# Router of a mixture of experts: the low parts of the tokens on VectorE alone, and fillers that read results of the ranking

## The chip, the cores and the metric

The kernel runs on one core of a Trainium2 chip. The metric is device time in microseconds (us) of one execution, as the median of several runs. Five engines work side by side, each through its own queue in order: TensorE (PE; its weight loads are PEld), VectorE (DVE), ScalarE (ACT), GpSimd (POOL) and SyncE (SP, which issues the DMAs).

## The reference, cut to what matters

Two blocks are computed one after the other on 256 tokens of 1024 features. The second block has two layers, and each layer ends with a mixture of 16 experts:

```
scores = sigmoid(t @ router_w);  biased = scores + router_bias
grp_score = sum of the two best biased scores in each of 4 groups of 4 experts
sel_group = argmax(grp_score);   top_idx = the two best experts in that group
gates = the unbiased scores of the two, divided by their sum
y = sum over experts of gates * (silu(gate) * up) @ w_down      (float32)
x = layer_norm(alpha * x + y)
```

The change lies in the router and in the gathers behind it. Both run once for each layer.

## The kernel before, in words

Products need float32 accuracy. An operand is split into a high part (`xnh`) and a low part (`xnl` = x - `xnh`), and each token is multiplied as high and low part.

The router is in `moe`. The normalised tokens stand in `zn`, [128 tokens, 2 token blocks t, 1024 features]. ACT makes the sigmoid's exponential, and then VectorE ranks in a chain of small instructions: `rank` over the experts of a group (`ed`, `erk`), the two best (`gs`, which is `found`), their sum by group (`gsc`, which is `summed`), `rank` over the four groups (`gd`, `grk`) and the selection `selb`. Three products on TensorE (lines 1406 to 1408, into the PSUM tile `po`) count the place of each token in the list of its expert, and VectorE makes from them `posm` and the slot matrices `sm`, one for each token block.

`to_gather` makes the operands of the gathers meanwhile: for each half c of the features and each t, ACT normalises `zn` (line 1364) and rounds it to `xnh` (1365), and one engine makes `xnl` (1366): GpSimd for c = 0, VectorE for c = 1. `first_ready` traces these four steps behind the slot matrices; its `issue_after` orders only instructions that stand on the same engine as the one it names. Behind them in program order stands `gates_and_rounds`: VectorE's `w` and `ws` (the gates), two products of TensorE into a further column range of `po` (1423, 1424), and `cmx`, VectorE's maximum of that (1426).

Each `gather` is eight products of 256 columns, `xnh` and `xnl` of two token blocks for two feature blocks, into one PSUM bank. The banks `st` and `w` have one buffer each and take turns: gather 0 uses `st`, which `po` holds until `cmx` has read it, and gather 1 uses `w`. Gathers 0 and 1 (features 0 to 511, c = 0) stand ahead of the first product of the experts (line 1632); gathers 2 and 3 (c = 1) lie between those products.

`busy(n)` issues n products that nothing reads (fillers, line 370). The router has `busy(30)`, two `busy(20)` and, behind the place products, `busy(14)`, all into bank `w`. None of these fillers waits for a result: the `issue_after` around them names an instruction of VectorE, so it does not order TensorE. The rows of statistics for the residual (line 435) lie between the fillers.

A planner fixes the order of each engine's queue before the run: of the instructions that its own cost figures take to be ready when an engine becomes free, it issues the one that comes first in the program. On the chip each engine works off its queue in that order.

Of the kernel before, what the change touches and what calls it, by code (L numbers as in the profile page):

```python
# [8 lines left out]
F32 = mybir.dt.float32  # L9
# [4 lines left out]
ALU = mybir.AluOpType  # L14
# [16 lines left out]
# ---------------------------------------------------------------- constants  # L31
def _constants():
    """Tables that depend on the shapes alone."""
# [4 lines left out]
    # rotate-half permutation for two stacked heads of 64  # L38
# [9 lines left out]
    # partial sums: rows 0 and 32 of one kind, 64 and 96 of another  # L48
# [26 lines left out]
    # trailing mean minus token, transposed: [token in, token out]  # L75
# [9 lines left out]
    # retention decay with the 1/sqrt(dk) of the keys, [key, query]  # L85
# [9 lines left out]
    # router helpers: iota - 512 over slots; the lead by which f comes before e in a group of four  # L95
# [11 lines left out]
def _cols(v):  # L107
    """[n*128] -> [128, n]: one column per block of 128 features."""
    return np.ascontiguousarray(np.asarray(v).reshape(-1, P).T)


def _panels(w, n):
    """[K, N] -> [N/n, 128, K/128, n], one contiguous block per panel."""
    w = np.asarray(w)
    K, N = w.shape
    return np.ascontiguousarray(w.reshape(K // P, P, N // n, n).transpose(2, 1, 0, 3))


def layout(inputs):
    """Only moves data: every array keeps its type and values."""  # L120
# [27 lines left out]
    pair = [0, 3, 1, 4, 2, 5]      # heads whose keys lie in the first / second half, in turn  # L148
# [24 lines left out]
# ---------------------------------------------------------------- kernel  # L173
def body(tc, A, out, dbg=None, stop=None):
# [3 lines left out]
    with ctx:  # L178
# [22 lines left out]
        # ------------------------------------------------------------ streams  # L201
# [12 lines left out]
        class weights:  # L214
            """fp32 weights [128, kb, n] from DRAM, split exactly into hi + lo, in two halves, of which
            some are made at once and the others when first used."""
# [23 lines left out]
            def at(self, k, a=None, b=None):  # L240
                """hi and lo of block k, columns a to b (all by default)."""
                for i, (k0, k1, c0, c1) in enumerate(self.cut):
                    if k0 <= k < k1 and (a is None or c0 <= a < c1):
                        c = slice(None) if a is None else slice(a - c0, b - c0)
                        return [t[:, k - k0, c] for t in self.make(i)]

        def mm3(o, wh, wl, xh, xl, first, last):
            """o += w^T x, both operands split; only lo*lo (below fp32) is left to rounding."""
# [7 lines left out]
        def xtile(tag, dt=F32R, name=None):  # L256
            """[128, KB, T + 2], or that much of another use."""
            return xp.tile([P, KB * (T + 2)], dt, name=name or tag, tag=tag)

        class Lead:  # L260
            """A tensor's split product with its gains, made block by block as its sums become known: the first
            products of the next step run on it, and what is the same for all features of a token is applied to them.
            Further columns, an even number, hold vectors that are added to each token, so that their products come along.
            The normalised tensor takes its place."""

# [15 lines left out]
            def products(self, ws, banks, ks):  # L281
                """Of the four blocks of columns of two panels, a bank each."""
# [10 lines left out]
        # ------------------------------------------------------------ start  # L293
# [28 lines left out]
        def ada(i):  # L322
            """Column i of the nine modulation vectors, a generator of a step per cut, or of two for the first."""
            mod = mods[:, i * 8:i * 8 + 8]
            for a, b in CUTS if i < 2 else [(a, a + 2) for a in range(0, KB, 2)]:
# [31 lines left out]
                if i % 3 == 1:   # scale: g * (1 + sc)  # L357
                    V.scalar_tensor_tensor(out=mod[:, c], in0=mod[:, c], scalar=1.0,
                                           in1=gains[:, i // 3 * 8 + a:i // 3 * 8 + b], op0=ALU.add, op1=ALU.mult)
                if i % 3 == 2:   # gate: 0.5 of the half steps, 0.5 of the sigmoid gates  # L360
# [5 lines left out]
        def busy(n, tag="w"):  # L366
            """Keeps the clock of the tensor engine up over a wait: products that nothing reads."""
            p = bank(tag, "busy")
            for i in range(n):
                PE.matmul(p[:, :P], identb, identb, start=True, stop=True)  # L370

        # ------------------------------------------------------------ norms
        class Sum:
            """Sums over all features of [128, T] blocks, as a column per token block."""
# [29 lines left out]
        class Norm:  # L404
            """Mean square over features of a transposed [128, KB, T] tensor, block by block."""
# [26 lines left out]
        def rows_to(rb, r):  # L432
            """Per-token columns [128, 2] as a row over all partitions: PSUM [128, T]."""
# [7 lines left out]
        def row(rb):  # L441
            """A row from PSUM in SBUF."""
# [4 lines left out]
        def lead_in(nrm, i, lead, ws, banks):  # L447
            """The first products, and the normalised tensor in place of their operand: rmsnorm(h) * scale + shift."""
# [9 lines left out]
        def norm_mod(rb, h, i, hi, lo):  # L458
            """hi + lo = rmsnorm(h) * scale + shift."""
# [7 lines left out]
        def first_rstd():  # L467
            """1 / rms of the input, as a row."""
# [24 lines left out]
        # ------------------------------------------------------------ FFN  # L493
        def begin(pool, start, pq, i, uh, ul, win):
            """The first three pairs of panels of the first FFN, one or two blocks of K at a time as the modulation comes in."""
# [115 lines left out]
        # ------------------------------------------------------------ rope of block 1  # L611
# [31 lines left out]
        def rotate(dst, src, cosT, sinT, pool, pq, raw=None, n=2):  # L643
            """dst [128, n, T] = rope of the two stacked heads in src, in PSUM unless raw has them too."""
# [10 lines left out]
        def proj_t(o, w, a, xh, xl, kb=KB):  # L655
            """o [128, T] = W[:, a:a+128]^T x^T."""
# [3 lines left out]
        def proj_k(banks, xh, xl, ks=range(KB)):  # L660
            """Several [128, T] products at once, the blocks of K outermost; a bank is a list of (o, w, a)."""
# [5 lines left out]
        def proj_n(o, w, xh, xl, t, kb=KB, k0=0, kt=None, cols=(None, None)):  # L667
            """o [tokens of block t, N] = x W."""
# [12 lines left out]
        def evac(dst, src):  # L681
            """PSUM to SBUF on the engine whose turn it is."""
# [6 lines left out]
        # ------------------------------------------------------------ softmax attention  # L689
        def softmax_rows(sc, n, nk, scale, pool, sink=None):  # L690
            """Joint softmax over [128, n, nk] scores in PSUM, one maximum per query."""
# [11 lines left out]
        # ------------------------------------------------------------ block 1 mixer  # L703
        def mixer(nrm, cosT, sinT, side, lead, then):
            with tc.tile_pool(name="mix", bufs=1, reuse_waits="tile") as pool, tc.tile_pool(name="mixp", bufs=1, reuse_waits="tile", space=bass.MemoryType.PSUM) as pq:
# [40 lines left out]
                # pooling  # L746
# [117 lines left out]
        # ------------------------------------------------------------ block 2  # L864
# [14 lines left out]
        rw = ctile([P, KB, 32], name="rw", pool=c2)     # router weights, and a column of ones for the sums  # L879
# [5 lines left out]
        def shift(means, after):  # L885
            """hT = alpha * hT - mean(alpha * hT)."""
# [9 lines left out]
        class LayerNorm:  # L896
            """Of hT + y, its sums taken on the tensor engine."""
# [10 lines left out]
            def add(self, m, y):  # L908
                """hT[:, m] += y."""
# [14 lines left out]
            def columns(self):  # L924
                """By token: the mean, the mean square, 1 / the deviation, and - the mean times that."""
# [12 lines left out]
            def finish(self, dst, g, b, each):  # L938
                """Block by block: dst = the normalised tensor; hT keeps what it was, less its mean."""
# [14 lines left out]
        def pair_softmax(s, scale, pool, sink=None):  # L954
            """Rows of two heads: s [128, 4, T], a bank per head, late queries in 0 and 2, early ones in 1 and 3."""
# [39 lines left out]
        def pair_values(pq, pool, p, pe, v, hi, lo):  # L995
            """hi + lo [128, T]: outputs of the two heads, transposed; v[i](t) are the values of key block t."""
# [13 lines left out]
        def first_weights(l, which, made=0):  # L1010
            """The first weights of a mixer."""
            return [weights(A["w_in_2"][l, i], KB, 256, "k", made=made) for i in which]

        def mixer2(l, lead, cols, first, normalise):
            with tc.tile_pool(name=f"mix2_{l}", bufs=1, reuse_waits="tile") as pool, \
# [54 lines left out]
                def latent(x, n, i, wc):  # L1070
                    """The rms norm of x, and then its transpose, split."""
# [22 lines left out]
                # latent queries, keys and values  # L1094
# [76 lines left out]
                # retention  # L1171
# [67 lines left out]
                # the router on the normalised sum z + y is linear in it but for the two statistics of a token  # L1239
# [30 lines left out]
                def after(m):  # L1270
                    """Block m of the sum: to token rows, and the products and sums over the features.
                    Blocks 0 to 6 a block in each quarter of the columns, the last one by token at once."""
# [53 lines left out]
        def moe(l, cols, zn, lg, GB, ahead):  # L1326
            col = lambda o, m: cols[:, o + m:o + m + 1]
            with tc.tile_pool(name=f"moe_{l}", bufs=1, reuse_waits="tile") as pool:
# [5 lines left out]
                # statistics of the tokens, and the router's logits  # L1334
# [21 lines left out]
                # the normalised tokens, without gain and shift, for the gathers  # L1356
# [3 lines left out]
                def to_gather():  # L1360
                    for c in range(2):
                        for t in range(2):
# [3 lines left out]
                            (G, V)[c].tensor_tensor(out=xnl[:, t, c_], in0=x, in1=xnh[:, t, c_].bitcast(F32), op=ALU.subtract)  # L1366
# [8 lines left out]
                def rank(x, n, name):  # L1375
                    """How many of the four come before each: larger, or equal and earlier. x [128, n*4]."""
# [24 lines left out]
                with tc.issue_after(found.ins):  # L1401
                    busy(20)
                with tc.issue_after(summed.ins):
                    busy(20)
# [11 lines left out]
                def gates_and_rounds():  # L1416
# [5 lines left out]
                    # more than CAP tokens for an expert: that many further rounds  # L1422
# [10 lines left out]
                with tc.tile_pool(name=f"moep_{l}", bufs=1, reuse_waits="tile", space=bass.MemoryType.PSUM) as pq:  # L1433
# [5 lines left out]
                    def residual_now():  # L1439
                        """hT = alpha * (its normalised value - the mean of that)."""  # L1440
# [61 lines left out]
        def experts(l, big, pool, nb, xn, posm, gates, acc, col, aside=None, loop=None):  # L1502
            """acc += the experts' outputs of the tokens in slots 0 to CAP-1 of each; two experts at a time,
            one in the left and one in the right half of the columns of the tensor engine."""
# [3 lines left out]
            def stage():  # L1508
                """Keeps the tensor engine to the order of the program."""
# [12 lines left out]
            def expert_weights(e, i, n):  # L1522
                """fp32 [128, 4, 512] of the gate and up weights for i = 0, 1; [128, 2, 1024] of the down weights for 2."""
# [298 lines left out]
```

## Time and profile before

| | us |
|---|---|
| median of 3 runs | 1182.7 |
| the three runs | 1182.67, 1182.70, 1187.75 |
| span of the profiled execution, first to last instruction | 1186.2 |
| PE busy | 1144.6 (96%) |
| PEld busy | 943.5 (80%) |
| DVE busy | 713.3 (60%) |
| ACT busy | 511.4 (43%) |
| POOL busy | 44.5 (4%) |

The profile gives the profiled execution's span but no other time of its own. Of the three runs only the one of 1187.75 us is long enough to contain a span of 1186.2 us. Spans count from the first instruction. The router of the first layer lies near 732 to 746 us and that of the second near 1024 to 1039 us. The mean granted clock of TensorE is 0.987, where 1.00 is 2.4 GHz and 0.50 is 1.2 GHz.

### The profile page before, as it was taken

How to read it: one execution, taken by the hardware profiler on the slowest of the kernel's cores; microseconds unless marked ns; L12 is line 12 of the kernel's file. 1: busy time of each engine (PE TensorE's matmuls, PEld its weight loads, DVE VectorE, ACT ScalarE, POOL GpSimd, SP SyncE). 2: the span in 40 equal slices, each digit the busy share in tenths (PEclk: the TensorE clock that was granted, in tenths of full speed). 3: DMA queues.
4: the chain of work that ended last, by engine and by line, in shares of the span. 5: the costliest groups of instructions: out<-in, count | busy, mean ns of one | idle time of the engine just before them, and what ended most of it. 6: DMA issues, size and time to landing. Idle time of an engine off the chain costs nothing. (4 is left out here: it accounts for less than half of the span.)

```text
span 1186.2 us, 20785 instructions
## 1 busy us (share of the span) xinstructions
PE 1144.6 (96%) x8495; PEld 943.5 (80%) x8495; DVE 713.3 (60%) x1410; ACT 511.4 (43%) x946; POOL 44.5 (4%) x53
## 2 busy tenths in 40 slices
PE   6999999999999999999999998999989999899995
PEld 4999999988888999999997878544458787844443
DVE  5698879777877775555677754621258864451114
ACT  4454445534534554444556434222247643322213
POOL 0000001000000200000120001000001000100000
PEclk9999999999999999999999999999989999999998
DMA  9788779738863455535572439599743334779941
GB/s 317 292 362 307 288 258 325 263 133 316 306 230 112 173 180 182 184 125 183 168 250 99 143 109 353 216 385 390 290 155 135 136 109 170 288 272 397 380 156 38
DMA packets 77354, 272.12 MB, mean 229 GB/s; under 512 B 7873, under 2 KB 10817, under 8 KB 62914
## 3 DMA queue, kind: packets, MB, share of 16 engines
q1 hardware_dynamic: 77250, 270.70, 62.8%
q8 instruction: 70, 1.15, 0.4%
q14 instruction: 34, 0.28, 0.1%
HBM read 269.63 MB, written 1.05 MB: 228 GB/s over the span
## 5 line engine op out<-in xcount | busy, mean ns | idle before, releaser
L254 DVE TENSOR_TENSOR hl<-raw,hl 128x1024 fp32r<-128x1024 f32 (+5 forms) x267 | 293.4, 1108 | 120.8 <-ACT hl L254 120.0
L254 ACT CAST hl<-raw 128x1024 fp32r<-128x1024 f32 (+5 forms) x267 | 254.0, 958 | 233.9 <-PE mm L251 172.2
L249 PE MATMUL mm<-xh,hl 128*128 128x256 f32 x896 | 255.2, 286 | 4.0 <-ACT xh L254 3.3
L251 PE MATMUL mm<-xh,hl 128*128 128x256 f32 x896 | 255.2, 285 | 0.0
L250 PE MATMUL mm<-xl,hl 128*128 128x256 f32 x896 | 253.4, 283 | 0.0
L249 PEld LDWEIGHTS mm<-xh,hl 128*128 128x128 f32 x896 | 169.6, 190 | 6.6 <-ACT xh L254 3.6
L250 PEld LDWEIGHTS mm<-xl,hl 128*128 128x128 f32 x896 | 170.4, 190 | 1.9 <-issue 1.9
L251 PEld LDWEIGHTS mm<-xh,hl 128*128 128x128 f32 x896 | 170.4, 190 | 1.0 <-issue 1.0
L1632 PE MATMUL gu<-hl,xg 128*64 128x512 f32 x208 | 101.8, 604 | 0.0
L249 PE MATMUL mm<-gh,hl 128*128 128x256 f32 x352 | 99.2, 282 | 0.0
L251 PE MATMUL mm<-gh,hl 128*128 128x256 f32 x352 | 99.2, 282 | 0.0
L250 PE MATMUL mm<-gl,hl 128*128 128x256 f32 x352 | 99.2, 282 | 0.0
L1632 PE MATMUL gu<-raw,xg 128*64 128x512 f32 x192 | 92.9, 603 | 0.0
L354 DVE SCALAR_TENSOR_TENSOR raw<-raw,cond 128x1024 f32<-128x1024 f32 x64 | 76.7, 1219 | 10.0 <-DMA raw<-in_w_ada_dram 10.0
L1668 DVE SCALAR_TENSOR_TENSOR ysl<-dn,gsl,ysh 128x512 fp32r<-128x512 f32 x32 | 23.9, 750 | 75.8 <-ACT ysh L1667 75.8
L250 PEld LDWEIGHTS mm<-gl,hl 128*128 128x128 f32 x352 | 67.0, 190 | 0.0
L249 PEld LDWEIGHTS mm<-gh,hl 128*128 128x128 f32 x352 | 67.0, 190 | 0.0
L251 PEld LDWEIGHTS mm<-gh,hl 128*128 128x128 f32 x352 | 67.0, 190 | 0.0
L1632 PE MATMUL gu<-rawe,xg 128*64 128x512 f32 x112 | 54.6, 604 | 0.0
L1619 DVE TENSOR_SCALAR xg<-ga,cols 128x256 f32<-128x256 f32 x32 | 17.4, 543 | 55.8 <-ACT xg L1618 55.8
L1667 ACT ACTIVATE ysh<-dn,gsl 128x512 fp32r<-128x512 f32 x32 | 22.0, 687 | 55.7 <-PE dn L1665 55.7
L1618 ACT ACTIVATE xg<-ga,cols 128x256 f32<-128x256 f32 x32 | 18.1, 565 | 60.9 <-PE ga L1615 55.0
(531 smaller groups left out, 2428.3 us busy)
## 6 DMA issues: line engine op xcount, KB each, us to landing
raw<-in_w_ffn_in_dram SPq DMA_DIRECT2D x41, 1024.0 KB, 4.9
raw<-in_w_ada_dram SPq DMA_DIRECT2D x34, 1024.0 KB, 6.2
raw<-in_w_in_dram SPq DMA_DIRECT2D x34, 1024.0 KB, 5.0
hl<-in_gate_up_dram SPq DMA_DIRECT2D x26, 1024.0 KB, 8.5
raw<-in_gate_up_dram SPq DMA_DIRECT2D x24, 1024.0 KB, 7.9
raw<-in_w_ffn_out_dram SPq DMA_DIRECT2D x32, 704.0 KB, 4.2
rawe<-in_gate_up_dram SPq DMA_DIRECT2D x14, 1024.0 KB, 8.2
raw<-in_w_out_dram SPq DMA_DIRECT2D x12, 1024.0 KB, 4.9
```

Of the source, the lines that this page charges most:

```text
L249: PE.matmul(o, wh, xh, start=first, stop=False)
L250: PE.matmul(o, wh, xl, start=False, stop=False)
L251: PE.matmul(o, wl, xh, start=False, stop=last)
L254: return S.copy(hi, x), V.tensor_tensor(out=lo, in0=x, in1=hi.bitcast(F32), op=ALU.subtract)
L354: V.scalar_tensor_tensor(out=w, in0=w, scalar=1.0, in1=cond, op0=ALU.mult, op1=ALU.mult, accum_out=mod[:, a + j:a + j + 1])
L1618: S.activation(out=xg[:, 2 * j], in_=p[:, :T], func=AF.Identity, scale=col(0, 2 * j), bias=col(8, 2 * j))
L1619: mark[0] = V.tensor_scalar(out=xg[:, 2 * j + 1], in0=p[:, T:], scalar1=col(0, 2 * j + 1), scalar2=col(8, 2 * j + 1), op0=ALU.mult, op1=AL ...
L1632: mm = PE.matmul(p[i * CAP:(i + 1) * CAP], xg[:, k, s], w[i][:, k % 4], start=(k == 0), stop=(k == KB - 1))
L1667: made = S.activation(out=ysh[:, c], in_=p, func=AF.Copy, scale=gc)
L1668: mark[0] = made, V.scalar_tensor_tensor(out=ysl[:, c], in0=p, scalar=gc, in1=ysh[:, c].bitcast(F32), op0=ALU.mult, op1=ALU.subtract)
```

## The change

`to_gather` makes all four `xnl` on VectorE. `busy` gets a new argument `since`: with it, the fillers begin with one float32 product of the identity with the tensor named, so that this product waits for the tensor. The two `busy(20)` in the router become one product that reads `gs` with 8 fillers, and one that reads `gsc` with 10, both into bank `st`. `gather` does the products of both feature blocks with `xnh` before those with `xnl`. The rest of the diff takes out comments and docstrings.

```
-        def busy(n, tag="w"):
+        def busy(n, tag="w", since=None):
             p = bank(tag, "busy")
+            if since is not None:
+                PE.matmul(p[:, :since.shape[-1]], ident, since, start=True, stop=True)
             for i in range(n):
                 PE.matmul(p[:, :P], identb, identb, start=True, stop=True)
...
-                            (G, V)[c].tensor_tensor(out=xnl[:, t, c_], in0=x, in1=xnh[:, t, c_].bitcast(F32), op=ALU.subtract)
+                            V.tensor_tensor(out=xnl[:, t, c_], in0=x, in1=xnh[:, t, c_].bitcast(F32), op=ALU.subtract)
...
                 busy(30)
                 with tc.issue_after(found.ins):
-                    busy(20)
+                    busy(8, "st", gs.rearrange("p a b -> p (a b)"))
                 with tc.issue_after(summed.ins):
-                    busy(20)
+                    busy(10, "st", gsc)
...
-                    for i in range(2):
-                        k = 2 * j + i
-                        for h in range(2):
-                            for t in range(2):
+                    for h in range(2):
+                        for t in range(2):
+                            for i in range(2):
+                                k = 2 * j + i
                                 mm = PE.matmul(p[:, i * T:(i + 1) * T], xn[h][:, t, k * P:(k + 1) * P], sm[:, t].rearrange("p e s -> p (e s)"),
-                                               start=(h + t == 0), stop=(h + t == 2))
+                                               start=(h + t + i == 0), stop=(h + t + i == 3))
```

## Rows read from the trace of the kernel before

**Rows 1.** Busy time by engine in five stretches (us, instructions in brackets), granted clock, DMA.
```profile
core 0: us, PE busy (x) PEld busy (x) DVE busy (x) ACT busy (x) POOL busy (x), PEclk, DMA share, GB/s
738.40:741.40 3.00, 0.00 (x0) 0.00 (x0) 2.81 (x6) 2.86 (x5) 2.45 (x2) 1.00 0.33 121
...
743.50:744.95 1.45, 1.45 (x9) 1.45 (x8) 1.45 (x4) 0.00 (x0) 0.00 (x0) 0.50 0.00 0
...
1035.30:1038.50 3.20, 3.16 (x15) 3.19 (x16) 2.41 (x11) 0.56 (x1) 0.00 (x0) 0.50 0.02 5
...
780.00:840.00 60.00, 60.00 (x338) 29.25 (x336) 12.22 (x22) 14.35 (x27) 0.00 (x0) 1.00 1.04 397
...
697.20:700.60 3.40, 2.69 (x18) 1.71 (x18) 0.45 (x2) 0.88 (x3) 1.64 (x1) 1.00 0.35 141
```

**Rows 2.** Timeline of TensorE, first layer: start, length, engine, line, operation, idle before.
```profile
732.92 0.62 PE L1278 MATMUL lgt<-rwg,hT 128*128 128x18 f32 x4
...
734.11 1.22 PE L370 MATMUL busy<-identb 128*128 128x128 bf16 x19
735.17 0.44 PE L435 MATMUL acc<-k_c_mats,nmu 128*128 128x128 f32 x2
735.45 1.28 PE L370 MATMUL busy<-identb 128*128 128x128 bf16 x20
...
741.40 0.17 PE L1406 MATMUL pos<-selb,ltb 128*128 128x16 bf16 x1 [3.01 <-DVE selb L1396]
...
741.48 1.63 PE L370 MATMUL busy<-identb 128*128 128x128 bf16 x14
...
743.51 0.77 PE L1615 MATMUL ga<-sm,xnh 128*128 128x256 f32 x2
...
746.22 0.64 PE L1632 MATMUL gu<-raw,xg 128*64 128x512 f32 x1
```

**Rows 3.** Timeline of TensorE, second layer.
```profile
1033.77 0.17 PE L1406 MATMUL pos<-selb,ltb 128*128 128x16 bf16 x1 [3.01 <-DVE selb L1396]
...
1035.34 0.77 PE L1615 MATMUL ga<-sm,xnh 128*128 128x256 f32 x2 [0.20 <-DVE ws L1418]
...
1038.82 0.64 PE L1632 MATMUL gu<-raw,xg 128*64 128x512 f32 x1
```

**Rows 4.** Timeline of VectorE, first layer.
```profile
738.20 0.19 DVE L1389 SCALAR_TENSOR_TENSOR gs<-erk,bi 128x32 f32<-128x32 f32 x1
...
738.43 0.19 DVE L1391 TENSOR_REDUCE gsc<-gs 128x8 f32<-128x32 f32 x1
738.65 1.03 DVE L1381 TENSOR_TENSOR gd<-gsc 128x32 f32<-128x32 f32 x1
739.71 1.19 DVE L1382 TENSOR_TENSOR gd<-gd,k_c_small 128x32 f32<-128x32 f32 x1
740.94 0.19 DVE L1384 TENSOR_REDUCE grk<-gd 128x8 f32<-128x32 f32 x1
...
741.88 0.76 DVE L1572 TENSOR_TENSOR sm<-k_c_small,posm 128x256 fp32r<-128x256 f32 x2
...
743.19 0.17 DVE L1426 TENSOR_REDUCE cmx<-pos 128x1 f32<-128x16 f32 x1 [0.45 <-PE pos L1424]
743.28 0.18 DVE L1418 TENSOR_REDUCE ws<-w 128x2 f32<-128x32 f32 x1
743.37 0.42 DVE L1572 TENSOR_TENSOR sm<-k_c_small,posm 128x256 fp32r<-128x256 f32 x1
743.70 1.29 DVE L1366 TENSOR_TENSOR xnl<-zn,xnh 128x512 fp32r<-128x512 f32 x2
```

**Rows 5.** Timeline of GpSimd, first layer.
```profile
738.36 2.49 POOL L1366 TENSOR_TENSOR xnl<-zn,xnh 128x512 fp32r<-128x512 f32 x2 [2.75 <-ACT xnh L1365]
```

**Rows 6.** Timeline of ScalarE, first layer.
```profile
737.68 1.12 ACT L1365 CAST xnh<-zn 128x512 fp32r<-128x512 f32 x2
...
740.13 1.12 ACT L1365 CAST xnh<-zn 128x512 fp32r<-128x512 f32 x2
```

**Rows 7.** Timeline of VectorE, second layer.
```profile
1034.92 0.18 DVE L1417 TENSOR_TENSOR w<-sc,selb 128x32 f32<-128x32 f32 x1
```

## The prediction

> **What bounds the kernel now.** I first read busy time by stretches. TensorE is the bound wherever the experts run: in the 60 us from 780 it is busy for all 60.00 at full clock while VectorE needs 12.22 [rows 1]. So a microsecond that the experts start earlier is a microsecond at the end, as long as nothing else holds them. In the router it is different. From 738.40 to 741.40 TensorE does nothing and VectorE, ScalarE and GpSimd are busy for 2.81, 2.86 and 2.45 us [rows 1]. The timeline of TensorE names what ends that wait: the place products at 741.40 had waited 3.01 us for the selection, and the second layer shows the same 3.01 us [rows 2, 3]. What counts is thus how early the first expert product starts, now 746.22 and 1038.82 [rows 2, 3]. On the way to it VectorE is the path: ranking, place products, slot matrices, `cmx`, then the gathers.
>
> Two things in that path are long. The two `gd` instructions, on 32 elements, take 1.03 and 1.19 us, where their neighbours take 0.19 and start 0.22 apart. They end at 739.68 and 740.90. GpSimd runs its two `xnl` from 738.36 to 740.85, so each `gd` ends where one of them does, while `gsc`, a reduction with one input, runs at 0.19 beside them [rows 4, 5]. And the clock falls behind the 3 us wait: 0.50 from 743.50 to 744.95, and 0.50 from 1035.30 to 1038.50 [rows 1], which is 1.2 GHz, in both layers just when the gathers run.
>
> **The change part by part.** All times are those of the first layer; the second lies 292.37 later (1033.77 - 741.40) [rows 2, 3].
>
> *No GpSimd in the ranking.* Both `gd` go to 0.22 apart: 738.65, 738.87, and `grk` at 739.09 instead of 740.94. That is 1.85 us a layer, and the place products could go at 739.55. The bounds are 0 (the wait has another cause) and 1.85.
>
> The Trainium skill, "SBUF — State Buffer", section "Who interferes with whom", says that a VectorE instruction with two SBUF inputs and a GpSimd instruction that reads SBUF exclude each other for the whole instruction. By that rule alone, with nothing else late, the sum would be 2 x 1.85 = 3.7 us less, 1179.0. The rows agree on the lock, but not that nothing else is late.
>
> *Fillers that wait.* Ahead of the place products TensorE now waits for `gs` (738.39, seen by TensorE at about 738.45), then does a float32 product and 8 fillers, then another and 10 fillers. A float32 product costs 0.28 (735.17 to the next start at 735.45; the smaller ones of line 1278 are four records, two products, in 0.62, so the other bound is 0.31). A filler costs 0.056 (19 from 734.11 to 735.17) [rows 2]. Together 0.28 + 0.45 + 0.28 + 0.56 = 1.57, so the place products go at 740.02, not 739.55: queued behind the fillers they lose 0.47 of the 1.85. At half clock the fillers cost double, 3.14. The gain so far is 741.40 - 740.02 = 1.38 us, and the slot matrices, which end at 742.64 now [rows 4], end at 741.26. The 40 fillers that go had run in time that TensorE waited anyway and give nothing back. The move from bank `w` to `st` queues nothing new: the place products use `st` behind them on the same engine.
>
> *Four `xnl` behind the slot matrices.* GpSimd's two go to VectorE at 1.29 for two, so VectorE has 2.58 us of them instead of 1.29 [rows 4]. Where they stand in its queue decides. In program order all four come ahead of `w`, `cmx` and `ws`. Now those three, and even a slot matrix of the next round, stand ahead of the two `xnl`, although `xnh` was ready at 741.25 on the chip [rows 4, 6]; so the planner took the second `xnh` to be ready only about when that slot matrix ran. The new two read the first `xnh`, ready at 738.80 [rows 6]; they come directly behind the slot matrices and fill 1.29 us, longer than the stretch from the end of the slot matrices to the end of that slot matrix in the second layer's order (`w` to gather 0.42, and the slot matrix 0.42 [rows 4, 7]; 0.84 together). By then the planner will hold the second `xnh` ready too, and put all four first. `w` then starts at 741.26 + 2.58 = 743.84. Gather 0 waits for `cmx`, because `po` holds its bank: in the second layer it starts 0.42 after `w` starts (1034.92 to 1035.34 [rows 3, 7]). So gather 0 starts at 744.26, against 743.51 now, and at 1036.63, against 1035.34: 0.75 and 1.29 later than before. The bounds of this part: with `w` first it would start at 741.68, with two `xnl` first at 742.97, with four at 744.26. I take four.
>
> *The gathers.* From gather 0 to the first expert product it is 2.71 us and 3.48 us now, of which 1.44 and 3.15 at half clock [rows 1 to 3]. Half of these is what the clock costs: 0.72 and 1.58. The rest, 1.99 and 1.90, is the price at full clock, 1.95 in the mean. The new order of the eight products in all 32 gathers changes neither their number nor their shapes; with all four `xnl` made before, it gains nothing. No row has that alternation. The two figures for the same two gathers differ by 0.09, 0.045 a gather, so I allow 32 x 0.045 = 1.4 us to either side and take 0.
>
> *The clock.* TensorE ends its fillers, place products and counts at about 741.05 (740.02 plus the 14 fillers, 0.78, plus 0.2) and then waits for gather 0 until 744.26, 3.2 us; now it waits 3.01 and loses the clock each time [rows 2, 3]. So I expect the loss again, right at the gathers. What it costs depends on when the clock falls: the two layers show 0.72 and 1.58, I take the mean, 1.15; the bounds are 0 and 1.95 (all of the gathers at half).
>
> The Trainium skill, "TensorE: Matmul & The Clock Gate", section "What's actually happening", states that the throttled state is the default and that activity releases it; the chip does not align its watch to the start of a program. By that rule the same kernel can pay differently from run to run, anything between the two bounds above; no run here shows it apart.
>
> **The sum.** First layer: 744.26 + 1.95 + 1.15 = 747.36 against 746.22, +1.14. Second: 1036.63 + 1.95 + 1.15 = 1039.73 against 1038.82, +0.91. Together +2.05, all of it passed on, since TensorE is the bound behind. Against the profiled execution's span of 1186.2 that is 1188.3; around it lie about 1.5 us if it was the run of 1187.75. The median of the three runs, 1182.7, is 5.05 less than that run; I put the same +2.05 on it: 1184.8. Its own range, by the clock's bounds, is 1182.4 to 1186.4.
>
> **The rivals.**
> 1. *`cmx` comes between the two pairs of `xnl`.* Gather 0 starts at 742.97, TensorE waits only 1.9 us and may keep its clock; a stretch with some 0.7 us of waiting kept 1.00 [rows 1], and 3 us did not. First expert products at 744.92 and 1037.29: -1.30 and -1.53, 1179.9. For it: the planner's times are its own. Against it: the order argued above.
> 2. *`cmx` comes directly behind the slot matrices, as in the second layer now.* Gather 0 starts at 741.68 on `xnh`; the second `xnl` ends at 741.26 + 0.42 + 1.29 = 742.97, two products (0.24) and gather 1 (0.97) follow: 744.2, and 1036.6. -2.0 and -2.25: 1178.4. Against it: `xnl` of the first half is ready earlier and stands earlier in the program.
> 3. *Slower: the clock falls already before the place products.* The fillers of `busy(30)` end at 735.33; three products of line 435 at 0.28 follow, so TensorE waits from about 736.3 to 738.45, 2.1 us, for `gs`. If that is enough, the fillers cost 3.14, place products go at 741.59, the slot matrices end at 742.83 and gather 0 starts at 745.83. With 1.95 and 1.15: 748.93 and 1041.30, +2.71 and +2.48, in all 1187.9; with all gathers at half clock 1189.5. It decides from the point where a wait of 2.1 us drops the clock, which lies between the waits seen.
> 4. *The ranking is not sped up.* `grk` stays at 740.94, the slot matrices end at 742.64, gather 0 starts at 745.64: with 1.95 and 1.15 it is +2.5 and +2.3, 1187.5. Against it: both `gd` end with GpSimd's instructions.
> 5. *As forecast, but the clock stays up*: 1182.4.
>
> **How the numbers follow.** Forecast 0.45, rival 1 0.23, rival 2 0.08, rival 3 0.09, rival 4 0.04, rival 5 0.11. The range takes in rivals 1 to 4, from 1178.3 to 1188.6; the order of the gathers (1.4) and a clock that is down longer lie in what is left out. A measurement of this kernel tells about 0.5%, 5.9 us, from no change: below 1176.8 lies only rival 2 with more gained from the gathers or the clock, 0.04; above 1188.6 the upper part of rivals 3 and 4, 0.09; between them 0.87.
>
> **What the profile would show.** Both `gd` at about 0.2 us and no `xnl` on GpSimd (else rival 4). Line 370 in two groups of 8 and 10 from 738.45 at 0.056 each (0.11 is rival 3). In VectorE's queue, four `xnl` between the slot matrices and `w` (two: rival 1; none: rival 2). Gather 0 near 744.3 and 1036.6, released by `cmx` or `ws`, and 0.50 in the stretch behind. I would be wrong if gather 0 started ahead of 743, or if the clock stayed at 1.00 through both gathers.

## The result, and the profile after

| | changed | before, in the same session |
|---|---|---|
| median, us | 1190.92 (8 runs, 1188.73 to 1194.44) | 1184.34 (8 runs, 1182.60 to 1188.38) |
| profiled execution, us | 1190.96, span 1189.1 | span 1186.2 |
| mean granted clock | 0.986 | 0.987 |
| GpSimd busy, us | 39.3 | 44.5 |

The ratio of the times is 1.0051, with an interval from 1.0032 to 1.0069: slower by about 6 us. The forecast had the sign right (+2.05) and the size wrong; 1190.92 lies above its range. Two executions, of 2116.95 us (r6) and 2774.26 us (r7), stand far outside all others of their kernels and are left out of the ratios below.

Spans mislead here. The router of the changed kernel begins 3.9 us earlier than that of before (its `gs` starts at 734.33, against 738.20 in [rows 4]), although nothing ahead of it was changed, and still the span is 2.9 us longer. The early clock goes with that: in the profile of before the granted clock is 0.50 from 28.4 to 34.5 us, where the changed kernel's has 1.00. Of the ten traces of this document three, before, e2 and r7, have such a stretch there and reach `gs` at 736.9 to 738.2; the other seven reach it at 733.6 to 734.5. So both traces are compared from `gs` of the first layer on. From there to the end before needs 448.0 us (1186.2 - 738.20) and the changed kernel 454.8 (1189.1 - 734.33): +6.8.

The timeline of VectorE of the changed kernel, first layer, answers to [rows 4]. Its columns are start, length, engine, line, operation, and the idle time before it with what ended that.

```profile
734.33 0.19 DVE L1391 SCALAR_TENSOR_TENSOR gs<-erk,bi 128x32 f32<-128x32 f32 x1
...
734.77 0.19 DVE L1383 TENSOR_TENSOR gd<-gsc 128x32 f32<-128x32 f32 x1
735.00 0.19 DVE L1384 TENSOR_TENSOR gd<-gd,k_c_small 128x32 f32<-128x32 f32 x1
...
735.45 0.19 DVE L1398 SCALAR_TENSOR_TENSOR selb<-grk,top 128x32 bf16<-128x32 f32 x1
736.76 0.19 DVE L1412 SCALAR_TENSOR_TENSOR posm<-selb,pos 128x32 f32<-128x32 bf16 x1 [1.13 <-PE pos L1410]
...
737.67 2.49 DVE L1368 TENSOR_TENSOR xnl<-zn,xnh 128x512 fp32r<-128x512 f32 x4
740.07 0.18 DVE L1419 TENSOR_TENSOR w<-sc,selb 128x32 f32<-128x32 f32 x1
740.18 0.17 DVE L1428 TENSOR_REDUCE cmx<-pos 128x1 f32<-128x16 f32 x1
740.29 0.18 DVE L1420 TENSOR_REDUCE ws<-w 128x2 f32<-128x32 f32 x1
```

Both `gd` take 0.19 us, where [rows 4] has 1.03 and 1.19. The ranking is done at 735.64, but `posm` waits 1.13 us more for TensorE. Then all four `xnl`, 2.49 us, stand ahead of `w`, `cmx` and `ws`.

The timeline of TensorE, first layer, answers to [rows 2]:

```profile
731.58 0.94 PE L372 MATMUL busy<-identb 128*128 128x128 bf16 x14
...
734.58 0.41 PE L370 MATMUL busy<-gs,k_c_mats 128*128 128x32 f32 x2 [1.33 <-DVE gs L1391]
734.82 0.61 PE L372 MATMUL busy<-identb 128*128 128x128 bf16 x8
735.49 0.39 PE L370 MATMUL busy<-gsc,k_c_mats 128*128 128x8 f32 x2
735.73 0.72 PE L372 MATMUL busy<-identb 128*128 128x128 bf16 x10
736.51 0.17 PE L1408 MATMUL pos<-selb,ltb 128*128 128x16 bf16 x1
...
740.49 1.19 PE L1617 MATMUL ga<-sm,xnh 128*128 128x256 f32 x4 [3.29 <-DVE ws L1420]
...
744.17 1.12 PE L1634 MATMUL gu<-raw,xg 128*64 128x512 f32 x1
...
746.83 0.75 PE L1617 MATMUL ga<-sm,xnh 128*128 128x256 f32 x4
```

And of the second layer, which answers to [rows 3]; its `gs` starts at 1030.84:

```profile
1031.08 0.41 PE L370 MATMUL busy<-gs,k_c_mats 128*128 128x32 f32 x2 [1.33 <-DVE gs L1391]
...
1033.30 0.17 PE L1408 MATMUL pos<-selb,ltb 128*128 128x16 bf16 x1
...
1037.29 1.19 PE L1617 MATMUL ga<-sm,xnh 128*128 128x256 f32 x4 [3.28 <-DVE ws L1420]
...
1043.70 0.75 PE L1617 MATMUL ga<-sm,xnh 128*128 128x256 f32 x4
```

The busy time by stretches shows the clock (third figure from the end: 1.00 is 2.4 GHz, 0.50 is 1.2 GHz). The first four stretches are of the first layer, the others of the second:

```profile
core 0: us, PE busy (x) PEld busy (x) DVE busy (x) ACT busy (x) POOL busy (x), PEclk, DMA share, GB/s
737.30:738.90 1.60, 0.00 (x0) 0.00 (x0) 1.60 (x5) 0.09 (x1) 0.00 (x0) 1.00 0.00 0
739.00:740.40 1.40, 0.00 (x0) 0.00 (x0) 1.40 (x6) 0.00 (x0) 0.00 (x0) 0.50 0.00 0
740.50:744.20 3.70, 3.70 (x18) 3.48 (x18) 1.77 (x10) 0.57 (x1) 0.00 (x0) 0.50 0.00 0
744.20:745.70 1.50, 1.50 (x5) 0.50 (x6) 0.54 (x1) 0.57 (x1) 0.00 (x0) 0.50 0.00 0
...
1032.60:1034.00 1.40, 1.07 (x12) 0.74 (x9) 0.40 (x2) 1.29 (x3) 0.00 (x0) 0.50 0.05 18
...
1041.00:1042.70 1.70, 1.70 (x5) 0.50 (x6) 0.54 (x1) 0.56 (x1) 0.00 (x0) 0.50 0.05 10
1042.80:1044.00 1.20, 1.20 (x8) 0.39 (x5) 0.00 (x0) 0.00 (x0) 0.00 (x0) 1.00 0.00 0
```

In the first layer the clock falls while TensorE waits for gather 0 and stays at 0.50 through both gathers and the first two blocks of expert products. In the second it is down already among the waiting fillers at 1032.6, ahead of the place products at 1033.30, and comes back only near 1042.8.

Because the low clock outlasts the gathers, the mark for the comparison is the start of the third gather (746.83 and 1043.70 above), behind the first four expert blocks. From there to the last expert product of the first layer both kernels take 127.51 us, so nothing of the router reaches further, and the new order of the gathers' products costs and gains nothing there. The 6.8 us are then:

| stretch | before | changed | difference |
|---|---|---|---|
| first layer, `gs` to third gather | 9.89 | 12.50 | +2.61 |
| last product of layer 1 to `gs` of layer 2 | 154.97 | 156.50 | +1.53 |
| second layer, `gs` to third gather | 10.12 | 12.87 | +2.75 |
| the rest | | | -0.15 |

### The profile page after: what moved, and what is told of

Same layout as the page of the kernel before. It is cut to its first block, busy times and chain, and to the rows that moved or that the text cites. A ratio compares the mean times of both kernels' runs of the same rounds, so it can differ in the third digit from the quotient of the medians.

```text
span 1189.1 us, 20713 instructions
## 1 busy us (share of the span) xinstructions
PE 1144.5 (96%) x8459; PEld 941.9 (79%) x8459; DVE 712.0 (60%) x1414; ACT 511.5 (43%) x946; POOL 39.3 (3%) x49
## 3 DMA queue, kind: packets, MB, share of 16 engines
q8 instruction: 69, 1.13, 0.4%
```

## The experiments

All compute the whole reference. The question was which of three things makes the loss: the four `xnl` ahead of `cmx`, the fillers that wait, or the clock. The marks of all runs, in us behind `gs` (first layer / second layer), and the ratio of their times to the kernel before, which was timed beside each group of runs (its medians: 1184.34 beside the changed kernel, 1186.64 beside e1 to e4, 1186.11 beside r5 to r7):

| kernel | place products | gather 0 | first expert product | third gather | time to before |
|---|---|---|---|---|---|
| before | 3.20 / 3.20 | 5.31 / 4.77 | 8.02 / 8.25 | 9.89 / 10.12 | 1 |
| before again | 3.20 / 3.21 | 5.34 / 4.78 | 9.02 / 8.31 | 10.95 / 10.19 | |
| changed | 2.18 / 2.46 | 6.16 / 6.45 | 9.84 / 10.13 | 12.50 / 12.87 | 1.0051 [1.0032, 1.0069] |
| e1, VectorE only | 1.36 / 1.36 | 5.34 / 5.34 | 8.92 / 8.82 | 10.79 / 10.69 | 1.0033 [1.0019, 1.0048] |
| e2, fillers only | 3.21 / 3.21 | 6.11 / 6.11 | 9.79 / 9.79 | 12.54 / 12.67 | 1.0041 [1.0026, 1.0056] |
| e3, gates first | 2.18 / 2.38 | 3.75 / 3.96 | 7.79 / 8.00 | 10.54 / 10.14 | 0.9998 [0.9984, 1.0012] |
| e4, cover | 2.18 / 2.18 | 6.16 / 6.16 | 8.22 / 8.21 | 10.09 / 10.08 | 0.9999 [0.9986, 1.0011] |
| r5 | 1.36 / 1.36 | 3.44 / 3.43 | 5.50 / 5.49 | 7.37 / 7.35 | 0.9958 [0.9944, 0.9972] |
| r6 | 1.36 / 1.36 | 3.44 / 3.43 | 5.68 / 5.67 | 7.54 / 7.54 | 0.9958 [0.9942, 0.9973] |
| r7, last fillers placed | 3.59 / 2.95 | 7.58 / 6.94 | 10.98 / 10.62 | 12.84 / 12.79 | 1.0043 [1.0023, 1.0063] |

**e1: the kernel before with `xnl` on VectorE alone.** The fillers stay as before.

```
-  (G, V)[c].tensor_tensor(out=xnl[:, t, c_], ...)
+  V.tensor_tensor(out=xnl[:, t, c_], ...)
```

> The kernel before with one part of the change alone: all four xnl on VectorE. Old fillers, old order of the gathers. Measure: from gs to the third gather (line 1615, just behind the first expert products), 9.89 and 10.12 us before, 12.50 and 12.87 in the changed kernel. Theory A (the queue of VectorE and the clock): selection early, place products 1.35 us behind gs instead of 3.20, but w, cmx, ws stand behind four xnl, gather 0 about 5.4 behind gs against 5.31 and 4.77, TensorE waits some 3 us ahead of it and loses its clock: 10.4 to 11.8, the kernel 1 to 4 us slower than before. Theory B (the fillers that wait are what makes the changed kernel slow): without them 9.9 or less, the kernel as before or up to 3.7 us faster.

One line of VectorE's timeline and two of TensorE's, first layer (`gs` at 733.96):

```profile
736.48 2.49 DVE L1366 TENSOR_TENSOR xnl<-zn,xnh 128x512 fp32r<-128x512 f32 x4
```

```profile
735.32 0.17 PE L1406 MATMUL pos<-selb,ltb 128*128 128x16 bf16 x1 [1.17 <-DVE selb L1396]
...
739.30 0.73 PE L1615 MATMUL ga<-sm,xnh 128*128 128x256 f32 x2 [2.60 <-DVE ws L1418]
```

The place products come 1.84 us earlier behind `gs` than before (1.36 against 3.20), what the prediction gave the ranking. Yet gather 0 comes at 5.34 as before: the four `xnl` eat all of it and the granted clock is still low there (0.51 from 739.30 to 742.80). So this half of the change gains nothing, and its time is 0.33% longer, as theory A had it. The third gather, 10.79 and 10.69, would explain 0.9 and 0.57 us of that, against the first profile of before, and -0.2 and 0.5 against the second; the profiled execution took 1185.99, 3.9 less than its kernel's median, so what the longer executions lose is not in this trace.

**e2: the kernel before with the waiting fillers alone.** GpSimd keeps its two `xnl`.

```
-  busy(20)
+  busy(8, "st", gs.rearrange("p a b -> p (a b)"))
...
-  busy(20)
+  busy(10, "st", gsc)
```

> The kernel before with the waiting fillers alone; GpSimd still makes two xnl during the ranking, old order of the gathers. Theory A: both gd stay at 1.03 and 1.19 us, the fillers end ahead of the selection and delay nothing (place products 3.20 behind gs); in VectorE's queue the two xnl now stand ahead of w and cmx, so gather 0 starts about 6.1 behind gs; third gather at 10.0 to 11.5, the kernel 0 to 3 us slower. Theory B (the fillers are what makes the changed kernel slow): place products later than 3.20 behind gs and third gather at 12 or more, the kernel 4 us or more slower.

The busy time by stretches (columns as above), VectorE's and TensorE's timeline, first layer (`gs` at 736.91):

```profile
737.00:740.00 3.00, 2.38 (x22) 1.94 (x22) 2.86 (x7) 2.96 (x5) 2.51 (x2) 0.71 0.35 128
...
743.00:746.70 3.70, 3.67 (x16) 3.48 (x16) 1.70 (x9) 0.56 (x1) 0.00 (x0) 0.50 0.00 0
```

```profile
737.36 1.04 DVE L1382 TENSOR_TENSOR gd<-gsc 128x32 f32<-128x32 f32 x1
738.43 1.20 DVE L1383 TENSOR_TENSOR gd<-gd,k_c_small 128x32 f32<-128x32 f32 x1
```

```profile
737.16 0.41 PE L369 MATMUL busy<-gs,k_c_mats 128*128 128x32 f32 x2 [1.34 <-DVE gs L1390]
...
740.13 0.20 PE L1407 MATMUL pos<-selb,ltb 128*128 128x16 bf16 x1 [0.54 <-DVE selb L1397]
...
743.03 0.76 PE L1616 MATMUL ga<-sm,xnh 128*128 128x256 f32 x2 [2.17 <-DVE ws L1420]
```

The third gather was expected at 10.0 to 11.5 behind `gs` and came at 12.54 and 12.67, and the kernel is 0.41% slower. These are the figures of theory B, but not by its way: the place products were on time (3.21), so they are not what is late. The clock was lost in both layers with the fillers that were to hold it: 0.71 in the stretch of the fillers, then 0.50. The wait ahead of them, 1.34 us, is little longer than the 1.17 in e1, which the clock outlasted; but here 18 fillers behind that wait stand for 40 without one. That this lost it is argued, not shown. The waits of 0.54 and 2.17 us came when the clock was already down (it is 0.50 from 738.3). Gather 0 is later too (6.11 against 5.31): two `xnl` (1.28 us from 741.42) now stand ahead of `cmx` (742.72), so this run changes VectorE's order as well as the fillers. Each half of the change alone loses, 0.33% and 0.41%, about as much as both together (0.51%; the intervals overlap).

**e3: the changed kernel with `gates_and_rounds` traced ahead of the `xnl`.**

```
+  gates_and_rounds()
   with tc.issue_after(sig.ins), tc.issue_after(ins):
       drain(split_x, 4)
-  gates_and_rounds()
```

> The changed kernel with gates_and_rounds traced ahead of the four xnl, so that cmx stands directly behind the slot matrices and frees the bank of gather 0. Theory A: gather 0 at 3.9 to 4.1 us behind gs (6.16 and 6.45 in the changed kernel), running on xnh while the xnl are made; third gather at 8.8 to 10.0, the kernel 4 to 8 us faster than the changed one and 0 to 2.6 us faster than before. Rival (it is the xnl themselves, not the bank behind cmx, that gather 0 waits for): gather 0 starts early but its xnl products wait, third gather at 11 or later.

One line of VectorE's timeline and two stretches, first layer (`gs` at 734.03):

```profile
737.47 0.17 DVE L1428 TENSOR_REDUCE cmx<-pos 128x1 f32<-128x16 f32 x1
```

```profile
735.00:737.80 2.80, 1.53 (x21) 1.14 (x18) 1.60 (x9) 2.08 (x4) 0.00 (x0) 0.82 0.05 20
737.80:741.80 4.00, 4.00 (x16) 3.51 (x16) 3.73 (x13) 0.56 (x1) 0.00 (x0) 0.50 0.00 0
```

Gather 0 comes 2.4 us earlier than in the changed kernel, as the order of VectorE's queue asks. But the clock is 0.50 all the same, from about 736.8 on (0.82 in the first stretch), although the last wait ahead of gather 0 is only 0.88 us. The third gather was expected at 8.8 to 10.0 and came at 10.54 and 10.14. The kernel is as fast as before, no more: 0.9998. In this trace an earlier gather alone does not save the clock.

**e4: the changed kernel with 56 more fillers behind the counts.**

```
   V.tensor_copy(nri, ...)            # the end of gates_and_rounds
+  busy(56)
```

> The changed kernel with 56 more fillers behind the two count products, in the time in which TensorE waits for gather 0, and nothing else. Theory A (the clock): gather 0 still 6.2 to 6.5 us behind gs, but the clock stays at 1.00 through gathers and first expert products: third gather at 10.0 to 10.3, the kernel 4 to 5 us faster than the changed one, 0 to 2 us slower than before. Rival (the gathers and first products are slow for another reason, the new order of the products or missing operands): third gather stays near 12.5.

TensorE's timeline and the stretches, first layer (`gs` at 734.50):

```profile
737.22 2.00 PE L372 MATMUL busy<-identb 128*128 128x128 bf16 x33
...
740.65 0.72 PE L1618 MATMUL ga<-sm,xnh 128*128 128x256 f32 x4 [0.93 <-DVE ws L1420]
...
742.72 0.64 PE L1635 MATMUL gu<-raw,xg 128*64 128x512 f32 x1
...
744.59 0.62 PE L1618 MATMUL ga<-sm,xnh 128*128 128x256 f32 x3
```

```profile
740.60:742.70 2.10, 2.05 (x16) 1.96 (x16) 1.51 (x11) 0.56 (x1) 0.00 (x0) 1.00 0.00 0
```

33 of the 56 stand behind the counts; the planner put the others into the groups, ahead of the ranking and ahead of the counts. Which of them hold the clock is not separated. This run prices the clock, and theory A held. Gather 0 starts at 6.16 as in the changed kernel, so VectorE's queue is the same, but the clock stays at 1.00: the two gathers take 2.07 us (740.65 to 742.72) instead of 3.68 (740.49 to 744.17), and the first four expert blocks 1.87 instead of 2.66. From gather 0 to the third gather it is 3.93 us against 6.34 and 6.41: 2.4 and 2.5 us a layer are the clock. The time is that of before, so what the changed kernel loses against before is the clock's, and what remains without it is a draw. It is no more than a draw although before runs part of its gathers at 0.50: the late gather 0 has eaten what the ranking gained.

**r5: what both halves could be worth.** The kernel before with `xnl` on VectorE and the new order in the gathers, but with the counts and `cmx` in a function of their own, traced ahead of the `xnl`, and 17 fillers more.

```
+  busy(17)                           # behind the two old busy(20)
...
+  with tc.issue_after(ins):
+      count()                        # the two count products and cmx
   with tc.issue_after(sig.ins), tc.issue_after(ins):
       drain(split_x, 4)
   gates_and_rounds()                 # w, ws, nr
```

> A version meant to be faster than both: all four xnl on VectorE and the new order of the gathers; the count products and cmx traced ahead of the xnl, w and ws behind them; the old fillers that wait for nothing, and 17 more of them ahead of the place products. Theory A (queue of VectorE and clock): place products 1.4 us behind gs, gather 0 at 3.3 to 3.5, clock at 1.00 through the gathers, third gather at 7.2 to 7.6 (9.89 and 10.12 before): 2.5 us a layer, the kernel 4 to 6 us faster than before. Rival (what bounds the start of the experts is something else, such as the xnl or the weights' arrival): gather 0 early, third gather at 9 or later, kernel as before.

VectorE's and TensorE's timeline, first layer (`gs` at 733.96):

```profile
736.48 0.68 DVE L1366 TENSOR_TENSOR xnl<-zn,xnh 128x512 fp32r<-128x512 f32 x1
737.08 0.17 DVE L1423 TENSOR_REDUCE cmx<-pos 128x1 f32<-128x16 f32 x1
737.16 1.88 DVE L1366 TENSOR_TENSOR xnl<-zn,xnh 128x512 fp32r<-128x512 f32 x3
```

```profile
737.40 0.72 PE L1620 MATMUL ga<-sm,xnh 128*128 128x256 f32 x4 [0.72 <-DVE cmx L1423]
```

`cmx` stands behind one `xnl` only, gather 0 starts 3.44 behind `gs`, the granted clock stays at 1.00 through both gathers, and the third gather comes at 7.37 and 7.35. The kernel is 0.42% faster than before, about 5 us, and so beats both, as theory A had it.

**r6: r5 without the 17 fillers and with the old order in the gathers.**

```
-  busy(17)
```

> The same without the 17 further fillers and with the old order of the gathers' products: against r5_best it prices these two. Theory A: gather 0 at 3.3 to 3.5 behind gs; its second product with xnl waits some 0.4 us for the second xnl; third gather at 7.6 where the clock stays up, and up to 9.2 where the wait of 1.2 us ahead of the place products drops it; 1 to 5 us faster than before. Rival (the new order of the products is what lets gather 0 run early): third gather 1.5 us or more later than in r5_best at full clock. TensorE has as many instructions as before; if their number sets the wait at the branch between the layers, that wait is 4.8 us as before, not the 5.8 of the changed kernel.

VectorE's and TensorE's timeline, first layer (`gs` at 733.60):

```profile
736.72 0.17 DVE L1422 TENSOR_REDUCE cmx<-pos 128x1 f32<-128x16 f32 x1
...
737.04 0.48 PE L1619 MATMUL ga<-sm,xnh 128*128 128x256 f32 x2 [0.70 <-DVE cmx L1422]
```

The third gather comes at 7.54 in both layers and the ratio is 0.9958 again. So the fillers and the order together are worth 0.17 to 0.19 us a layer. From e1 this run differs only in where the counts and `cmx` stand, and there the third gather came at 10.79 and 10.69 and the ratio was 1.0033. So that position, with the clock which it keeps at 1.00, is worth 3.2 us a layer and makes the loss of e1 a gain. The place products wait 1.17 us for the selection, as in e1, and the clock does not fall. TensorE's wait between the layers was expected to be 4.8 us, if the number of its instructions sets it; it was 5.07.

**r7: the changed kernel with the 14 fillers put back behind the place products,** by letting them wait for `posm`.

```
-  busy(14)
+  busy(14, "w", posm[:, 0])
```

> The changed kernel with the 14 fillers that were meant to stand behind the place products made to read posm, so that they do; the planner had moved them ahead of the ranking. Theory (the clock stays down twice as long in the changed kernel because these 14 no longer follow the place products): gather 0 still 6.2 to 6.5 behind gs, but the stretch at half clock is 3.4 us long as before instead of 6.8 and 10.2; third gather at 10.8 to 11.5, the kernel 2 to 3 us faster than the changed one. Rival (what counts is the wait just ahead of gather 0, still 2 us): third gather at 12 to 12.9, the kernel as the changed one.

TensorE's timeline and one stretch, first layer (`gs` at 737.44):

```profile
737.78 0.61 PE L370 MATMUL busy<-gs,k_c_mats 128*128 128x32 f32 x2 [2.16 <-DVE top L1396]
738.20 1.04 PE L372 MATMUL busy<-identb 128*128 128x128 bf16 x8
...
745.02 1.19 PE L1617 MATMUL ga<-sm,xnh 128*128 128x256 f32 x4 [1.34 <-DVE ws L1420]
```

```profile
738.00:741.00 3.00, 2.91 (x22) 2.49 (x23) 0.64 (x4) 2.49 (x5) 0.00 (x0) 0.50 0.20 76
```

My theory fell. The rival's figures came, but not by its way. Without the 14 ahead of the ranking, TensorE waits 2.16 us for the product that reads `gs` instead of 1.33 (the line names `top`, which VectorE makes right behind `gs`), the granted clock is 0.50 from the first fillers on, these start 0.107 apart instead of 0.056, and the place products come 3.59 behind `gs`. So the clock was gone some 7 us ahead of gather 0, whose own wait was only 1.34. The third gather is at 12.84 and 12.79, later than in the changed kernel's first layer.

**Before again,** one more profile of the unchanged kernel.

> The kernel before, profiled once more. From gs to the third gather some 9.9 to 10.1 us and the wait at the branch between the layers 4.8 us, if the profiles so far are typical; what differs between this and the first profile of it is what one profile can differ by without a change.

The stretches of the first layer (`gs` at 733.98):

```profile
739.40:743.10 3.70, 3.70 (x19) 3.48 (x20) 2.77 (x12) 0.56 (x1) 0.00 (x0) 0.50 0.00 0
```

The same code lost more here: the clock is at 0.50 through both gathers and had been down since 736.4, where in [rows 1] only 743.50 to 744.95 of the gathers was slow, and the third gather comes 10.95 behind `gs` instead of 9.89 (9.9 to 10.1 expected). So a layer of the kernel before has no fixed price either, and a difference of 1 us a layer between two traces is no proof by itself.

## Why the prediction was wrong

**Right: the lock.** Both `gd` went to 0.19 as forecast, and in e2, where GpSimd keeps its work, they stay at 1.04 and 1.20. The rule of the Trainium skill, "SBUF — State Buffer", section "Who interferes with whom", agrees with that. The 3.7 us which it would give by itself did not come, since `cmx` was late next, as the sum assumed; in r5, where it is not and the clock stays up too, the kernel gains about 5.

**Right: four `xnl` ahead of `w`, `cmx` and `ws`.** Gather 0 was forecast 6.06 behind `gs` (744.26 - 738.20) and came at 6.16 and 6.45, behind a wait of 3.29 and 3.28 (3.2 forecast). Rivals 1 and 2, in which `cmx` stands earlier, did not happen. Rival 2 is close to what r5 builds.

**Wrong in size: the clock, the step that failed.** I took 1.15 us a layer with bounds of 0 and 1.95 ("all of the gathers at half"). It cost 2.4 and 2.5 (e4 against the changed kernel). Two things were off. The clock fell not "right at the gathers" but before them, during the wait in the first layer and among the fillers in the second, so that both gathers ran slowly: +1.6 us by the same pair of runs. And the upper bound ended with the gathers, while the low clock ran on into the first expert blocks: +0.79 in the first layer, +0.87 in the second. Rows of before had shown only a low clock that returned within the gathers, and I took that for the most it can do. Even there the clock fell earlier than I read: in the first layer of before it is 0.53 over the stretch ahead of the gathers.

```profile
741.40:743.50 2.10, 2.10 (x21) 2.10 (x21) 1.36 (x7) 0.00 (x0) 0.00 (x0) 0.53 0.01 4
```

So the 0.72 was what the gathers got of a low clock that had begun two microseconds ahead of them, and nothing in the rows bounded its end by theirs. The Trainium skill, "TensorE: Matmul & The Clock Gate", section "What's actually happening", says that the same kernel can pay differently from run to run; the two profiles of before agree, with 9.89 and 10.95.

**Wrong: where `busy(14)` goes.** I left the 14 fillers behind the place products. They wait for nothing, and the new fillers no longer use bank `w`: they run at 731.58, ahead of the ranking, and in e2, where only the fillers are changed, at 734.15. That the bank is the reason is argued, not tested. So TensorE did nothing from the counts (the last starts at 737.03) to gather 0. That wait came out as forecast (3.29 against 3.2) by luck, because the place products were later. Gather 0 at 6.16 is luck in part too: with the 14 where I had put them (r7) it comes at 7.58 and 6.94. That is rival 3, which had 7.63 (745.83 - 738.20), with the wait of 2.16 us that it named (2.1) and fillers at 0.107. In the second layer of the changed kernel the clock also fell ahead of the place products, behind a wait of only 1.33.

**Mis-sized: the fillers.** 1.93 us from 734.58 to the place products at 736.51 in the first layer, against 1.57, and 2.22 in the second, where they run partly at 0.50. A filler does cost 0.056, but each new tile in bank `st` starts only when the last product in the tile before it has been written: the eight end at 735.43 and the next begins at 735.49, the ten end at 736.45 and the place products begin at 736.51. A product into another tile does not wait so: in [rows 2] the one at 735.17, into `acc`, starts before the 19 fillers ahead of it have ended (735.33).

**By the sum.** To the third gather I had, with 1.87 for the four blocks as before, +1.14 and +0.91. Measured is +2.61 and +2.75. The 1.47 missing in the first layer are 0.10 for gather 0, 0.58 for the gathers (3.68 against 1.95 + 1.15) and 0.79 for the expert blocks; the 1.84 in the second are 0.39, 0.58 and 0.87. The level to which I added the sum was less certain than the sum: the unchanged kernel's median was 1182.7, 1184.34, 1186.64 and 1186.11 in four sets of runs, the first of which is part of the second. 1.6 of the 6.1 us from 1184.8 to 1190.92 are that level.

**The 1.53 us between the layers.** Before again needs 155.91 there, so the same code varies by 0.94, and 0.59 is left against that profile. 1.0 of the 1.53 is TensorE's wait for a DMA at line 249, 4.80 before and 5.81 after. The rest is the clock again. When that wait ends, the clock is at 0.50, for 5.0 us more in the profile of before (883.3 to 888.3) and for 6.1 in the changed kernel's (883.1 to 889.2); half of the difference is 0.55. The two terms hold beyond this pair: the stretch less its wait less half of the low clock behind it is 147.6 to 147.7 us in nine of the ten traces (146.8 in e4, which has a second low stretch at 907 to 911). What sets the wait stays open. It is 4.80 and 5.28 in the two profiles of before, 4.84 in e1, 5.07 to 5.33 in r5, r6 and e4, and 5.79 to 5.91 in e2, e3 and r7. All four kernels at the upper end have the waiting fillers, but e4 has them too, at 5.21. No run settled it.

**Rivals 4 and 5.** The ranking was sped up, so 4 did not happen. The clock that stays up is e4: it took 56 more fillers, 33 of them in the wait, and comes out at 0.9999 of before, where 5 had 1182.4 of 1182.7.

## What to carry to other kernels

Removing a lock pays only as far as the moved work does not queue ahead of the small instruction that frees the next resource: here a 0.17 us maximum, placed behind one `xnl` instead of four, turned +0.33% (e1) into -0.42% (r6). Fillers help only where they run: in e4 56 more, 33 of them in the wait ahead of gather 0, kept the clock, and in r7 the 14 that were moved away from ahead of the ranking lost it there. A filler that waits for nothing goes where the planner puts it, not where it is written; look in the trace where it ran. Compare traces from an event ahead of the change to one behind its last effect, and profile the unchanged kernel twice before reading 1 us into a difference.

## What was not expected of the hardware

- A short wait with few fillers behind it can cost the clock, and need not. In the changed kernel's second layer it was at 0.50 from 1032.6 on, behind a wait of 1.33 us and amid the fillers; in the first layer, with the same rows, it held until the wait for gather 0. In e1 and r6 a wait of 1.17 us, with 40 fillers ahead of it and 14 behind, did not cost it in any of the four layers.
- The low clock does not end with the wait: 739.0 to 745.7 in the first layer of the changed kernel, and 1032.6 to 1042.7 in the second, with TensorE busy without a gap from 1037.3 on.
- GpSimd's lock held one `gd` until the end of each of its instructions (1.03 and 1.19 us), but not the reduction `gsc` beside it (0.19 in [rows 4]).
